# Attention scores over 64 rows: two heads in TensorE's row halves in place of stacked high and low parts

## The chip, the cores and the metric

One core of one Trainium2 chip runs the whole program. The metric is the device time of one execution in microseconds (us). The core has a matrix engine (TensorE, "PE" in the profile, with its weight loads listed apart as "PEld"), three engines for elementwise work (VectorE or DVE, ScalarE or ACT, GpSimd or POOL), and SyncE (SP), which issues most transfers. Matmuls read their operands from SBUF, which has 128 rows (partitions), and write into the banks of PSUM. In a matmul the "stationary" operand is loaded into the array first (a weight load), then the "moving" operand streams through; the contraction runs over the rows.

## The reference

The program is three transformer layers over 256 tokens of width 1024, all in float32. The change touches three groups of eight heads with 64 channels each: the sixteen heads of the neighborhood attention of the second layer (two groups), and the eight heads of the dilated attention of the third layer. Cut to what matters:

```python
# second layer: 16 heads of 64 channels
s = jnp.einsum('bqhd,bikhd->bhqik', qblk, kblk).astype(jnp.float32) * scale + bias
s = jnp.where(colmask[:, None, :], s, -jnp.inf)
p = jax.nn.softmax(s.reshape(B, H, GRID_W, kr * GRID_W), axis=-1)
...
# third layer: 8 heads of 64 channels, three causal patterns of windows
scores = jnp.einsum('bnqrhe,bnkrhe->bnrhqk', qb, kk).astype(jnp.float32) * scale
...
p = jnp.exp(scores - lse[..., None]).astype(v.dtype)
o = jnp.einsum('bnrhqk,bnkrhe->bnqrhe', p, vv)
```

With 256 tokens each head's scores are a 256 x 256 matrix, a product over 64 channels, with a bias or mask on it.

## The kernel before

**Two parts for each number.** TensorE multiplies in a rounded float32 form (F32R). To keep precision, an operand is split into a high part (rounded) and a low part (the rest): ACT writes the high part, DVE subtracts it from the source and writes the low part (`hilo`, `split`). A projection with weights then takes three matmuls: high by high, high by low, low by high.

**Tiles.** A projection (`proj_t`, `proj_sum`) leaves 256 output channels by 256 tokens as two tiles of 128 rows in `t_sum`. 128 rows are the 64 channels of two heads, a pair: head 0 in rows 0 to 63, head 1 in rows 64 to 127.

**Scores, stacked.** `q_stack` turns a pair's rows into one tile per head whose 128 rows are the 64 channels of the high part and, in the other row half, those of the low part. It takes two ACT and two DVE instructions of 64 rows for each projection. `k_stack` does the same for K, but with the high part in both halves of one tile and the low part in both halves of another; the second copies are made by four transfers that POOL issues (`nc.gpsimd.dma_start`). In `scores_stacked` a matmul of 128 rows then gives (Qhigh + Qlow) by Khigh, a second one (Qhigh + Qlow) by Klow, into the same place of PSUM. With two tiles of 128 queries a head has four matmuls. In the causal group the first query tile has only 128 keys.

**The three groups.** `heads8` runs them: c0 and c1 in `layer_odd`, d in `mixer`. It makes two projections each for K and Q, one for V, and hands `scores` to `pair_heads`, which puts three kinds of steps into a background list for each head: first (scores and softmax), second (softmax weights, transposed by TensorE), third (the product with V, for a pair). `pace` takes steps from that list while projections are written out, so that attention work stands among projection work. The product with V and all else in these groups is not changed; nor are the groups a, b and the memory heads, which use `q_stack`, `k_stack` and `scores_stacked` or `scores_full` as before.

**What sets the order.** No instruction is issued as the code is written. `Plan.record` notes each operation with its dependencies and an estimated duration from `Plan.cost`; `Plan.order` then plays the program through, and each time an engine is free it takes the ready operation with the lowest priority number. The number is the operation's place in the code plus a shift: `SHIFT = {("tensor", "mm"): 100, ("vector", "wl"): -20}` puts TensorE's projection matmuls (outputs in the PSUM tiles "mm") 100 places back. Score matmuls write to "at" tiles and get no shift. Where the two numberings meet, score and projection matmuls are taken in turn, one by one. TensorE runs its instructions in that order; `Plan.issue` emits all of them from one line, so every row of the profile bears this line (L284 before). PSUM has four "at" tiles and four "mm" tiles; a shared pool "b4" has 24 slots in SBUF, from which the Q and K tiles come too.

Of the kernel before, what the change touches and what calls it, by code (L numbers as in the profile page):

```python
# [11 lines left out]
F32R = mybir.dt.float32r  # L12
# [4 lines left out]
P = 128  # L17
S = 256
# [11 lines left out]
class Plan:  # L30
# [100 lines left out]
    def cost(self, engine, method, args, kwargs, outs, ins):  # L131

        if method == "dma_start":
            o = outs[0]
            nbytes = 4 * math.prod(o.shape)
            return (1040.0 if engine == "gpsimd" else 50.0), 950.0, nbytes
        n = math.prod(outs[0].shape[1:])
        sbuf = not any(self.mine(v) and self.tiles[v.tensor.name]["pool"].space == bass.MemoryType.PSUM for v in ins)
        col = kwargs.get("bias") is not None or isinstance(kwargs.get("scale"), bass.AP)
        accum = kwargs.get("accum_out") is not None  # L140
        if engine == "tensor":
            slow = 4.0 if args[1].dtype == F32 and method == "matmul" else 2.0 if method == "transpose" else 1.0
            if self.mine(args[2]) and args[2].tensor.name == "t_warm":
                slow = 2.0
            return max(n * slow, 256) / 2.4 + 2.4, 0.0, 0
        if engine == "scalar":
            return n / 1.2 + (93 if sbuf else 51) + 94 * col + 93 * accum, 0.0, 0
        if engine == "vector":
            if method == "tensor_reduce":
                n = math.prod(ins[0].shape[1:])  # L150
            if method in ("tensor_scalar", "tensor_copy") and sbuf:
                n /= 2
            ptr = method in ("tensor_scalar", "scalar_tensor_tensor") and isinstance(args[2], bass.AP)
            return n / 0.96 + 68 + 62 * ptr + 10 * accum, 0.0, 0
        if ALU.pow in args:
            return 300.0 + 165 * n, 0.0, 0
        if method == "memset":
            return 40.0 + n, 0.0, 0
        return 130.0 + 2.2 * n, 0.0, 0
# [148 lines left out]
class Kernel:  # L308
# [419 lines left out]
    def scores_stacked(self, q, kh, kl, spans):  # L728
# [6 lines left out]
            nc.tensor.matmul(o, q[:, t * P:(t + 1) * P], kl[:, k0:k0 + n], start=False, stop=True)  # L735
        return sc

    def scores_full(self, parts):

        sc = self.psum("at")  # L740
        for t in range(2):
            ts = slice(t * P, (t + 1) * P)
            for i, (qh, ql, kh, kl) in enumerate(parts):
                self.mm3(sc[:, t, :], qh[:, ts], ql[:, ts], kh, kl, i == 0, i == len(parts) - 1)
        return sc
# [357 lines left out]

    def heads8(self, tag, w_in, cq, ck, cv, hT, bias, out, causal=False, before=None):

        qs, ks = [], []
        for i in range(2):
            ks.append(self.k_stack(self.proj_t(w_in, ck + 256 * i, hT)))
            qs.append(self.q_stack(self.proj_t(w_in, cq + 256 * i, hT), -0.125))
        v = self.v_heads(self.proj_n(self.wide(w_in, 0, KT, cv), KT, 512, hT))  # L1110
        spans = ((0, P), (0, S)) if causal else self.FULL

        def scores(h):
            i, j = divmod(h, 4)
            return self.scores_stacked(qs[i][:, j, :], ks[i][0][:, j, :], ks[i][1][:, j, :], spans)

        if before:
            before()
        self.pair_heads(tag, 8, scores, bias, None, v, out, causal)
# [371 lines left out]
```

## Time and profile before

| | |
|---|---|
| time, median of 3 runs | 780.11 us (779.42 to 781.4) |
| the profiled execution's own time | 779.68 us |
| its span, first to last instruction | 777.9 us |
| TensorE busy | 763.1 us, 4320 matmuls recorded |
| DVE, ACT, POOL busy | 620.0, 536.8, 74.7 us |
| granted TensorE clock | 0.995 of full speed |

A group's row reads: line, engine, operation, output<-inputs by the program's names, form, count, then busy time and mean duration, then idle time before it and what ended that. In a matmul's row "128*128" are rows and columns of the stationary operand, and "128x256" is the moving one. The duration of a matmul is longer than the time for which it holds TensorE, since matmuls overlap: the pace is read from one start to the next. Timeline rows give the start, the duration of the piece, and "xN" for N alike in a row.

### The profile page before, as it was taken

What the parts mean: (1) busy time and instruction counts of PE and PEld (TensorE: products, weight loads), DVE (VectorE), ACT (ScalarE), POOL (GpSimd) and SP (SyncE); (2) the same over time, 40 slices, a digit from 0 to 9 for tenths busy, and PEclk for the clock granted to TensorE, in tenths of its full rate; (3) what the DMA queues carried; (4) which work ended last, traced back from release to release, by engine and by line L of the source; (5) the groups of instructions that cost most, each with busy time, mean ns of one, the idle gap of its engine ahead of it and who ended that gap; (6) DMA issues with size and microseconds to landing.
All of it is one profiled execution on the core that took longest, in us unless ns stands there. A gap on an engine that the chain in (4) does not pass through costs nothing.

```text
span 777.9 us, 11758 instructions
## 1 busy us (share of the span) xinstructions
PE 763.1 (98%) x4320; PEld 661.2 (85%) x4320; DVE 620.0 (80%) x1127; ACT 536.8 (69%) x1046; POOL 74.7 (10%) x105
## 2 busy tenths in 40 slices
PE   8989999999999999999999999999999999999996
PEld 7678898888888888888888898799989888888885
DVE  5999998998779889979988889976677655565554
ACT  6697987876679669757787787465556765556552
POOL 0640010000001421132011100100000000000000
PEclk9999999999999999999999999999999999999998
DMA  7796546445558855765348645356535565655631
GB/s 231 244 285 216 162 127 227 138 137 176 184 186 260 237 159 157 210 202 190 115 156 242 191 120 193 105 179 217 181 118 164 177 185 180 215 191 187 210 115 54
DMA packets 109989, 140.48 MB, mean 181 GB/s; under 512 B 3779, under 2 KB 81539, under 8 KB 109932
## 3 DMA queue, kind: packets, MB, share of 16 engines
q1 hardware_dynamic: 104460, 131.64, 52.5%
q0 software_dynamic: 5472, 8.10, 4.7%
q8 instruction: 34, 0.56, 0.3%
q14 instruction: 23, 0.19, 0.1%
HBM read 134.98 MB, written 1.06 MB: 175 GB/s over the span
## 4 chain that ended last, share of the span: by engine, by line
PE 86%; DVE 5%; issue 3%; POOL 2%; ACT 2%; DMA 1%; SPq 0%; POOLq 0%; DVEq 0%; ACTq 0%
PE t_mm L284 64%; PE t_at L284 22%; DVE t_wl L284 2%; DVE t_y L284 1%; POOL t_rrs L284 1%; POOL t_rstd L284 1%; DMA t_xT<-in_x_t_dram 1%; POOL t_ks L284 1%; ACT t_wh L284 0%; DVE t_xs L284 0%; DVE t_p L284 0%; DVE t_x L284 0%; ACT t_p L284 0%; ACT t_xg L284 0%; ACT t_mT L284 0%
## 5 line engine op out<-in xcount | busy, mean ns | idle before, releaser
L284 DVE TENSOR_TENSOR t_wl<-t_raw,t_wh 128x1024 fp32r<-128x1024 f32 (+1 forms) x237 | 288.8, 1219 | 72.6 <-ACT t_wh L284 70.9
L284 ACT ACTIVATE t_wh<-t_raw 128x1024 fp32r<-128x1024 f32 (+1 forms) x237 | 250.4, 1058 | 74.2 <-PE t_mm L284 61.3
L284 PE MATMUL t_mm<-t_mT,t_wh 128*128 128x512 f32 (+1 forms) x512 | 181.6, 394 | 0.4 <-ACT t_wh L284 0.4
L284 PE MATMUL t_mm<-t_mT,t_wl 128*128 128x256 f32 x496 | 131.9, 284 | 0.0
L284 PE MATMUL t_mm<-t_wh,t_yh 128*128 128x512 f32 x288 | 113.5, 394 | 0.0
L284 PE MATMUL t_mm<-t_wh,t_yl 128*128 128x512 f32 x288 | 112.9, 393 | 0.0
L284 PE MATMUL t_mm<-t_wl,t_yh 128*128 128x512 f32 x288 | 112.7, 391 | 0.0
L284 PEld LDWEIGHTS t_mm<-t_mT,t_wh 128*128 128x128 f32 x512 | 93.7, 188 | 14.0 <-ACT t_wh L284 0.8
L284 PEld LDWEIGHTS t_mm<-t_mT,t_wl 128*128 128x128 f32 x496 | 93.4, 189 | 6.5 <-DVE t_wl L284 0.3
L284 PE MATMUL t_at<-t_mT,t_wh 128*128 128x512 f32 (+1 forms) x256 | 85.7, 382 | 0.0
L284 ACT COPY t_sum<-t_mm 128x256 f32<-128x256 f32 x97 | 36.0, 371 | 55.6 <-PE t_mm L284 55.1
L284 PE MATMUL t_mm<-t_wh,t_gh 128*128 128x256 f32 (+2 forms) x256 | 65.9, 339 | 1.5 <-ACT t_wh L284 1.5
L284 PE MATMUL t_at<-t_mT,t_wl 128*128 128x256 f32 x240 | 63.8, 280 | 0.0
L284 PEld LDWEIGHTS t_mm<-t_wh,t_yl 128*128 128x128 f32 x288 | 54.1, 188 | 11.1
L284 PEld LDWEIGHTS t_mm<-t_wl,t_yh 128*128 128x128 f32 x288 | 54.1, 188 | 10.8
L284 PEld LDWEIGHTS t_mm<-t_wh,t_yh 128*128 128x128 f32 x288 | 54.1, 188 | 10.5 <-ACT t_yh L284 0.2
L284 PE MATMUL t_mm<-t_hT,t_wh 128*128 128x512 f32 x168 | 61.8, 400 | 1.0 <-DVE t_sum L284 1.0
L284 ACT ACTIVATE t_p<-t_p,t_st 128x256 f32<-128x256 f32 (+1 forms) x111 | 52.6, 493 | 9.6 <-DVE t_st L284 9.4
L284 POOL TENSOR_TENSOR t_rstd<-t_rstd,t_mhalf 128x2 f32<-128x2 f32 (+1 forms) x12 | 13.3, 1107 | 457.3 <-DVE t_rstd L284 457.3
L284 PEld LDWEIGHTS t_at<-t_mT,t_wh 128*128 128x128 f32 x256 | 45.8, 188 | 6.8
L284 DVE TENSOR_TENSOR t_sum<-t_mm,t_sum 128x256 f32<-128x256 f32 x97 | 40.8, 421 | 13.5 <-ACT t_sum L284 12.7
L284 PEld LDWEIGHTS t_mm<-t_wh,t_gh 128*128 128x128 f32 x256 | 45.1, 194 | 5.9 <-ACT t_wh L284 1.7
(177 smaller groups left out, 1389.1 us busy)
## 6 DMA issues: line engine op xcount, KB each, us to landing
t_raw<-in_w_in_odd_dram SPq DMA_DIRECT2D x20, 1024.0 KB, 5.2
t_raw<-in_w_up_dram SPq DMA_DIRECT2D x16, 1024.0 KB, 5.7
t_raw<-in_w_down_dram SPq DMA_DIRECT2D x16, 1024.0 KB, 5.0
t_raw<-in_w_in_dram SPq DMA_DIRECT2D x12, 1024.0 KB, 5.5
t_raw<-in_w_in_even_dram SPq DMA_DIRECT2D x10, 1024.0 KB, 5.1
t_raw<-in_w_mem_kv_dram SPq DMA_DIRECT2D x8, 1024.0 KB, 5.2
t_raw<-in_w_out_even_dram SPq DMA_DIRECT2D x6, 1024.0 KB, 5.6
t_raw<-in_w_out_odd_dram SPq DMA_DIRECT2D x6, 1024.0 KB, 5.3
```

The costliest lines, as they stand in the source:

```text
L284: f(*[self.real(v) for v in args], **{k: self.real(v) for k, v in kwargs.items()})
```

## The change

The three groups of `heads8` no longer stack. Q and K of a pair are split by `hilo` as they lie, high and low in tiles of their own, one ACT and one DVE instruction of 128 rows for each projection; Q takes two slots of the pool and K two, for all eight heads. The transfers that POOL issued for the second copies of K are gone in these groups (24 of them; the eight for a and b stay). `scores_pair` computes two heads at once: for each query tile and each of three terms (Qhigh Khigh, Qhigh Klow, Qlow Khigh) one matmul over rows 0 to 63 for the first head, and one over rows 64 to 127 for the second, alternating, each head into its own PSUM tile. The term low by low is no longer computed. A pair has twelve matmuls of 64 rows in place of eight of 128; both heads' scores are made in the step of the first head, and the second head's wait in `ready`. `Plan.cost` gets a price for such a matmul: half of the columns, at least 128.

```diff
+            if args[1].dtype == F32R and args[1].shape[0] == 64:
+                slow = 0.5
+            return max(n * slow, 128 if slow < 1 else 256) / 2.4 + 2.4, 0.0, 0
...
+    def scores_pair(self, qh, ql, kh, kl, spans):
+
+        sc = [self.psum("at") for _ in range(2)]
+        terms = ((qh, kh), (qh, kl), (ql, kh))
+        for t, (k0, n) in enumerate(spans):
+            for i, (x, y) in enumerate(terms):
+                for e in range(2):
+                    rows = slice(64 * e, 64 * e + 64)
+                    self.nc.tensor.matmul(sc[e][:, t, :n], x[rows, t * P:(t + 1) * P], y[rows, k0:k0 + n], start=i == 0,
+                                          stop=i == 2)
+        return sc
...
     def heads8(self, tag, w_in, cq, ck, cv, hT, bias, out, causal=False, before=None):
 
-        qs, ks = [], []
+        q, k = ([self.slot([P, 4, S], n) for _ in range(2)] for n in ("qs", "ks"))
         for i in range(2):
-            ks.append(self.k_stack(self.proj_t(w_in, ck + 256 * i, hT)))
-            qs.append(self.q_stack(self.proj_t(w_in, cq + 256 * i, hT), -0.125))
+            for x, c0, scale in ((k, ck, 1.0), (q, cq, -0.125)):
+                self.hilo(*(t[:, 2 * i:2 * i + 2, :] for t in x), self.proj_t(w_in, c0 + 256 * i, hT), scale)
...
+        ready = {}
+
         def scores(h):
-            i, j = divmod(h, 4)
-            return self.scores_stacked(qs[i][:, j, :], ks[i][0][:, j, :], ks[i][1][:, j, :], spans)
+            if h not in ready:
+                ready[h], ready[h + 1] = self.scores_pair(*(t[:, h // 2, :] for t in q + k), spans)
+            return ready.pop(h)
```

**Where the instructions go.** On TensorE, at the scores of the first heads of c0 (names are output<-moving,stationary; t_ks and t_qs are the K and Q tiles, t_mm a projection; the listing does not show how many rows a matmul has), before:

```order
L284 MATMUL t_at_3143<-t_ks_2837,t_qs_2937 128x256
L284 MATMUL t_at_3143<-t_ks_2848,t_qs_2937 128x256
L284 MATMUL t_at_3143<-t_ks_2837,t_qs_2937 128x256
L284 MATMUL t_at_3143<-t_ks_2848,t_qs_2937 128x256
L284 MATMUL t_mm_3150<-t_mT_2368,t_wh_3087 128x512
```

and now, in the same place:

```order
L286 MATMUL t_at_3125<-t_ks_2851,t_qs_2961 128x256
L286 MATMUL t_at_3127<-t_ks_2851,t_qs_2961 128x256
L286 MATMUL t_at_3125<-t_ks_2851,t_qs_2944 128x256
L286 MATMUL t_at_3127<-t_ks_2851,t_qs_2944 128x256
L286 MATMUL t_mm_3137<-t_mT_2368,t_wh_3071 128x512
L286 MATMUL t_at_3125<-t_ks_2862,t_qs_2944 128x256
L286 MATMUL t_mm_3137<-t_mT_2368,t_wl_3080 128x256
L286 MATMUL t_at_3127<-t_ks_2862,t_qs_2944 128x256
L286 MATMUL t_mm_3137<-t_mT_2368,t_wh_3071 128x512
```

A head's four matmuls stood together here; of the pair's twelve, eight stand together (the last four of them are shown), and the other four stand one by one between matmuls of 128 rows.

On TensorE too, later in c0, at the scores of the last pair:

```order
L286 MATMUL t_at_3447<-t_ks_2851,t_qs_2944 128x256
L286 MATMUL t_mm_3385<-t_wh_3340,t_yl_2812 128x512
L286 MATMUL t_at_3450<-t_ks_2851,t_qs_2944 128x256
L286 MATMUL t_mm_3399<-t_wh_3340,t_yh_2794 128x512
L286 MATMUL t_at_3447<-t_ks_2862,t_qs_2944 128x256
L286 MATMUL t_mm_3399<-t_wl_3358,t_yh_2794 128x512
L286 MATMUL t_at_3450<-t_ks_2862,t_qs_2944 128x256
L286 MATMUL t_mm_3399<-t_wh_3340,t_yl_2812 128x512
```

Here the two heads of a pair (tiles 3447 and 3450) take turns with the output projection of the memory heads, so the two row halves are never next to each other. Over all three groups the 144 score matmuls of 64 rows stand in 70 runs: 56 alone, and 14 runs of 2 to 12.

More of the change, by code (lines that the diff above doesn't have):

```diff
@@ L144, in cost @@
                 slow = 2.0
-            return max(n * slow, 256) / 2.4 + 2.4, 0.0, 0
+            if args[1].dtype == F32R and args[1].shape[0] == 64:
+                slow = 0.5
+            return max(n * slow, 128 if slow < 1 else 256) / 2.4 + 2.4, 0.0, 0
         if engine == "scalar":
```

## Prediction

> **What bounds the kernel now.** I read the profile's page first, then the waits of TensorE, the windows of the three stretches in which the groups of eight heads run, and last the timeline of TensorE and of its weight loads. First the page: its head, the busy time of TensorE, and the chain that ended last.
>
> ```profile
> span 777.9 us, 11758 instructions
> PE 763.1 (98%) x4320; PEld 661.2 (85%) x4320; DVE 620.0 (80%) x1127; ACT 536.8 (69%) x1046; POOL 74.7 (10%) x105
> ...
> PE 86%; DVE 5%; issue 3%; POOL 2%; ACT 2%; DMA 1%; SPq 0%; POOLq 0%; DVEq 0%; ACTq 0%
> ```
>
> TensorE (PE) is busy 98% of the span and carries 86% of the chain. A busy share says little of matmuls that are pipelined, so the waits of TensorE come next (waiter, releaser, us in total, times, longest).
>
> ```profile
> PE t_mm L284 <- ACT t_wh L284: 1.9, 2, 1.5
> PE t_mm L284 <- DVE t_wl L284: 1.6, 3, 1.0
> ...
> PE t_at L284 <- DVE t_qs L284: 0.2, 1, 0.2
> PE t_at L284 <- DVE t_y L284: 0.2, 1, 0.2
> ```
>
> The largest is 1.9 us; no row names the K tiles (t_ks) or their copies, and the Q tiles (t_qs) cost 0.2 us once. Now the windows of the stretches with the projections, scores and softmax of the groups c0, c1 and d (start:end, length, busy time of each engine).
>
> ```profile
> 222.00:290.00 68.00, 68.00 (x400) 59.68 (x399) 59.20 (x119) 52.10 (x107) 17.47 (x21) 1.00 0.72 215
> 290.00:360.00 70.00, 70.00 (x403) 60.94 (x402) 61.72 (x128) 51.15 (x104) 16.61 (x21) 1.00 0.67 194
> 408.00:478.00 70.00, 69.82 (x411) 61.05 (x412) 62.61 (x138) 55.55 (x125) 4.79 (x9) 1.00 0.63 186
> ```
>
> TensorE is busy 207.8 of these 208 us at the full clock (1.00). So what the change is worth there is what it does to TensorE's stream, and hardly anything else.
>
> **What leaves ACT, DVE and POOL.** The rows of the K and Q tiles in this part of the span (count, duration in ns min/median/max), and the rows of qm, which is split already in the form that the change adopts:
>
> ```profile
> L284 PE MATMUL t_at<-t_ks,t_qs x96: 220/281/336, 271.0 to 461.7; 128*128 128x256 f32 x80, 128*128 128x128 f32 x16
> L284 POOL DMA_DIRECT2D t_ks<-t_ks x24: 581/581/628, 242.5 to 429.7; - x24
> L284 ACT ACTIVATE t_ks<-t_sum x12: 617/628/632, 241.6 to 427.3; 64x512 fp32r<-64x512 f32 x12
> L284 DVE TENSOR_TENSOR t_ks<-t_sum,t_ks x12: 676/684/692, 242.7 to 428.6; 64x512 fp32r<-64x512 f32 x12
> ...
> L284 ACT ACTIVATE t_qs<-t_sum x12: 616/627/630, 248.7 to 434.0; 64x512 fp32r<-64x512 f32 x12
> L284 DVE SCALAR_TENSOR_TENSOR t_qs<-t_sum,t_qs x12: 684/686/690, 250.1 to 435.5; 64x512 fp32r<-64x512 f32 x12
> ...
> L284 ACT ACTIVATE t_qm<-t_sum x4: 618/625/635, 62.0 to 220.0; 128x512 fp32r<-128x512 f32 x4
> L284 DVE SCALAR_TENSOR_TENSOR t_qm<-t_sum,t_qm x4: 674/682/686, 63.0 to 220.8; 128x512 fp32r<-128x512 f32 x4
> ```
>
> Twelve projections lose half their splitting: ACT 24 x 0.63 becomes 12 x 0.63, 7.5 us less; DVE 24 x 0.685 becomes 12 x 0.68, 8.2 us less; POOL loses 24 DMA issues, 14 us. I take 0 for all three on the path, since TensorE waits 0.2 us for these tiles and there is 0.2 us of idle to win back in 208. That is also the most that this part can gain, and it cannot lose anything. Two fewer slots of the shared pool per group (four tiles for six) go the same way.
>
> **What TensorE's own stream costs.** Before, 24 heads have four score matmuls each, 96. Now twelve pairs have twelve each, 144: three terms, two query tiles, two heads. So 48 more instructions, each with its own weight load. What one costs is read from starts. The timeline of TensorE where a head's four run in a row, and where four others run one by one among projection matmuls (start, us, form):
>
> ```profile
> 271.03 0.64 PE L284 MATMUL t_at<-t_ks,t_qs 128*128 128x256 f32 x4
> 271.50 0.40 PE L284 MATMUL t_mm<-t_mT,t_wh 128*128 128x512 f32 x1
> ...
> 272.91 0.28 PE L284 MATMUL t_at<-t_ks,t_qs 128*128 128x256 f32 x1
> 273.03 0.40 PE L284 MATMUL t_mm<-t_mT,t_wh 128*128 128x512 f32 x1
> 273.27 0.28 PE L284 MATMUL t_at<-t_ks,t_qs 128*128 128x256 f32 x1
> 273.39 0.28 PE L284 MATMUL t_mm<-t_mT,t_wl 128*128 128x256 f32 x1
> ```
>
> Four start to start take 0.47 us, 0.12 each, and the lone ones too (272.91 to 273.03): today a score matmul costs the same in a row as alone. The pace of the weight loads is read where four short matmuls stand in a row early in the span (four loads and the load behind them, then TensorE's own rows; the loads are 128 columns wide, like every load of the scores):
>
> ```profile
> 21.41 0.52 PEld L284 LDWEIGHTS t_at<-t_p,t_ones 128*128 128x128 f32 x4 [0.86 <-DVE t_p L284]
> 21.85 0.19 PEld L284 LDWEIGHTS t_mm<-t_wh,t_gh 128*128 128x128 f32 x1
> ...
> 21.41 0.71 PE L284 MATMUL t_at<-t_p,t_ones 128*128 128x128 f32 x4 [0.43 <-DVE t_p L284]
> 21.88 0.47 PE L284 MATMUL t_mm<-t_wh,t_gh 128*128 128x512 f32 x1
> 22.19 0.39 PE L284 MATMUL t_mm<-t_wl,t_gh 128*128 128x512 f32 x1
> ```
>
> Four loads take 0.44 us, so one per 0.11 us is the load path's pace. It is the floor for a matmul that brings a load of its own, whatever its stream takes; the 16 narrow causal ones (128 columns) also stand at about 0.11. Before: 80 x 0.12 + 16 x 0.11 = 11.3 us. After, at the load pace: 144 x 0.11 = 15.8 us, **+4.5 us**. Bounds: 0.12 each would be +6.0; if the two row halves load and stream at once, a pair costs one place, 0.055 each, 7.9 us, a gain of 3.4. Nothing in this trace shows two halves at work at once, while loads of 128 columns one behind the other are in every window, so I take 0.11.
>
> The second cost is the change of the array's shape, from 128 rows to 64 and back. One place of this trace has a matmul of another shape, the small one of the window bias (33 rows, 8 columns, recorded as two passes). Its group, an ACT instruction that the reading needs, and the timeline of the loads and of TensorE around it:
>
> ```profile
> L284 PE MATMUL t_at<-t_tanh,t_rb 33*8 33x512 f32 x2 | 1.0, 586 | 0.7 <-POOL t_sink L284 0.7
> ...
> 19.41 1.06 ACT L284 ACTIVATE t_wh<-t_raw 128x1024 fp32r<-128x1024 f32 x1 [0.24 <-DMA t_raw<-in_w_in_even_dram]
> ...
> 26.23 0.12 PEld L284 LDWEIGHTS t_at<-t_tanh,t_rb 33*8 33x8 f32 x2 [1.08 <-POOL t_sink L284]
> ...
> 26.26 1.01 PE L284 MATMUL t_at<-t_tanh,t_rb 33*8 33x512 f32 x2 [0.69 <-POOL t_sink L284]
> 27.20 0.50 PE L284 MATMUL t_mm<-t_wh,t_gh 128*128 128x512 f32 x1
> 27.54 0.40 PE L284 MATMUL t_mm<-t_wl,t_gh 128*128 128x512 f32 x1
> ...
> 27.20 0.19 PEld L284 LDWEIGHTS t_mm<-t_wh,t_gh 128*128 128x128 f32 x1 [0.86 <-ACT t_hT L284]
> ```
>
> The pair of passes lasts 1.01 us and one of them 0.59, so they start 0.42 apart and stream until 26.26 + 2 x 0.42 = 27.10. The next load starts at 27.20, 0.1 us behind the end of the stream; at 21.85 above, between matmuls of one shape, it began 0.27 us before the recorded end of the row of four (21.41 + 0.71). And the matmul behind it holds TensorE for 0.34 us (27.20 to 27.54) where one of 512 columns takes 0.24 (273.03 to 273.27), so 0.1 of load lies open. One change of shape: 0.1 + 0.1 = 0.20 us. The profile names ACT as the releaser of that load, but the tile t_wh that this matmul reads was written by the ACT instruction at 19.41, so I read the 0.86 us as the wait for the passes to leave the array.
>
> How many such changes there are follows from the order. Of the 144 instructions 56 stand alone between matmuls of 128 rows, as the second excerpt on the change shows, and 88 stand in 14 rows of 2 to 12. That makes 70 runs, 140 changes. The way in is not shown by any row: the load at 26.23 waited for POOL. From 0 to the price of the way out, I take the latter, since the array holds matmuls of the other shape in both directions: 140 x 0.20 = **+28.0 us**. Upper bound for a change: the whole tail of a matmul (0.28 recorded less 0.12 of pace) and a whole recorded load of 0.19, 0.35 us, +49. Lower: 0.
>
> The Trainium skill says, in "TensorEngine Tiling (Array Packing)", Key Properties, that changing the tiling mode, and not only the tile, drains TensorE. It gives no price; by it the way in costs as well, and the sum is the one that I take. The one change of shape in this trace agrees (0.1 us behind the end of the stream).
>
> The sum against the profiled execution of 779.68 us: +4.5 + 28.0 = +32.5, 812.2; the median of the runs is 780.11, 0.43 above it, so **812.6 us**.
>
> **Rivals.** (1) The change of shape costs half: only one direction empties the array, or the open load is all. 4.5 + 140 x 0.10 = +18.5, 798.6 us. For it: the way in is unseen. Against it: the order puts as many ways in as out.
>
> (2) It costs nothing and the loads still go one by one: +4.5, 785 us. For it: the row at 26.26 differs also in its 8 columns and its float32 type, so its emptying may belong to the columns. Against it: the row of four ahead of 21.85 is float32 too (both operands are float32 in the code) and shows none.
>
> (3) It costs nothing and the halves run side by side inside the 14 rows: 42 pairs and 4 left over at 0.11 and 56 lone ones at 0.12, 11.8 us for 11.3: 780.5 us, no change. The 56 lone ones have no partner to run beside.
>
> (4) The other side: half the rows make load and stream half as long for every one of the 144, lone ones too, and the change of shape is free: 144 x 0.06 = 8.6 us for 11.3, -2.7, 777.4 us. This is what the planner's new cost for such matmuls says. It decides only if a change of shape costs less than 2.7 / 140 = 0.02 us, a tenth of what the trace shows once. The Trainium skill speaks for (3) and (4) where it says, in "TensorE: Matmul & The Clock Gate", The mechanism, that loads overlap running matmuls when the row groups differ; no run here shows it so far.
>
> **How the numbers follow.** The forecast has 0.58 (0.05 of that above 820 us, toward the upper price), (1) 0.15, (2) 0.10, (3) 0.08, (4) 0.09. The range 781 to 820 leaves out (4), half of (3) and that upper end. A measurement of this kernel tells about 0.3%, 2.3 us, from no change: the forecast, (1) and (2) are slower, 0.83; (3) the same, 0.08; (4) faster, 0.09.
>
> **What would show it.** Right: lone score matmuls of 64 rows take 0.4 to 0.5 us from the matmul before to the one after, instead of 0.12; the loads around them start only behind the end of the stream; rows of eight or twelve step at about 0.11 us; the three stretches grow by some 10 us each and the rest of the span stays. The load groups of t_at<-t_ks,t_qs count 144, ACT and DVE are 7 to 8 us lighter, and TensorE's waits name no new tile. Wrong: lone ones at 0.12 us with loads ahead of them (rivals 2 to 4), starts of two halves a few ns apart (3), or a new wait of TensorE for score banks (t_at), since a pair now takes two of four at once, which would add to any of these.

## The result and the profile after

The changed kernel takes 813.48 us (median of 4 runs, 812.86 to 814.21); before it was 779.76 us beside it. The ratio is 1.0428, with a 95% interval of 1.0411 to 1.0445: 34 us slower. The profile's page of the changed kernel, its head, the busy times and the granted clock in 40 slices:

```profile
span 812.1 us, 11774 instructions
...
PE 796.9 (98%) x4368; PEld 670.9 (83%) x4368; DVE 618.5 (76%) x1117; ACT 528.6 (65%) x1032; POOL 58.8 (7%) x81
...
PEclk9999999999999999999999789999999999999998
```

TensorE is "busy" for 34 us more with only 48 more matmuls, 0.7 us for each. DVE, ACT and POOL are lighter (618.5 for 620.0, 528.6 for 536.8, 58.8 for 74.7). New are the 7 and the 8 in the row of the clock, some 450 to 475 us into the span.

The score matmuls and their loads in the three groups, in the view by tile (durations min/median/max):

```profile
L286 PEld LDWEIGHTS t_at<-t_ks,t_qs x144: 182/183/285, 271.7 to 493.3; 64*128 64x128 f32 x144
L286 PE MATMUL t_at<-t_ks,t_qs x144: 268/331/579, 271.7 to 493.3; 64*128 64x256 f32 x120, 64*128 64x128 f32 x24
```

They are the 144 that were forecast, now of 64 rows ("64*128"). Where lone ones stand between projection matmuls, TensorE's timeline in c0 reads (start, duration, form):

```profile
273.12 0.38 PE L286 MATMUL t_mm<-t_mT,t_wl 128*128 128x256 f32 x1
273.43 0.38 PE L286 MATMUL t_at<-t_ks,t_qs 64*128 64x256 f32 x1
273.74 0.50 PE L286 MATMUL t_mm<-t_mT,t_wh 128*128 128x512 f32 x1
274.17 0.38 PE L286 MATMUL t_at<-t_ks,t_qs 64*128 64x256 f32 x1
274.48 0.38 PE L286 MATMUL t_mm<-t_mT,t_wl 128*128 128x256 f32 x1
```

and the loads of weights in the same place:

```profile
273.43 0.18 PEld L286 LDWEIGHTS t_at<-t_ks,t_qs 64*128 64x128 f32 x1
273.74 0.19 PEld L286 LDWEIGHTS t_mm<-t_mT,t_wh 128*128 128x128 f32 x1
274.17 0.18 PEld L286 LDWEIGHTS t_at<-t_ks,t_qs 64*128 64x128 f32 x1 [0.25 <-issue]
274.48 0.19 PEld L286 LDWEIGHTS t_mm<-t_mT,t_wl 128*128 128x128 f32 x1
```

Every step that took 0.12 us before takes 0.31 (273.12 to 273.43, 273.43 to 273.74), and that of 512 columns 0.43 (273.74 to 274.17) where it took 0.24. Each load starts in the same hundredth of a microsecond as its own matmul, so nothing was loaded ahead. Against 0.12 that is 0.19 for each change of the array's shape, on the way in as on the way out. As an estimate, a step of 0.31 is a load of 0.11 (the pace of the loads before), a stream of 0.11 and 0.09 that is left for emptying; no row shows load and emptying apart.

Where eight stand in a row, the same timeline shows something else:

```profile
271.39 0.39 PE L286 MATMUL t_mm<-t_wh,t_mT 128*128 128x512 f32 x1
271.71 0.74 PE L286 MATMUL t_at<-t_ks,t_qs 64*128 64x256 f32 x8
272.38 0.50 PE L286 MATMUL t_mm<-t_mT,t_wh 128*128 128x512 f32 x1
```

Eight take 0.67 us, with the load and the emptying in it; at 0.11 each they alone would take 0.88. The two row halves do run side by side.

### The profile page after: what moved, and what is told of

It is laid out like the page before. It is cut to its first block, busy times and chain, and to the rows that moved or that the text cites. A ratio compares the mean times of both kernels' runs of the same rounds, so it can differ in the third digit from the quotient of the medians.

```text
span 812.1 us, 11774 instructions
## 1 busy us (share of the span) xinstructions
PE 796.9 (98%) x4368; PEld 670.9 (83%) x4368; DVE 618.5 (76%) x1117; ACT 528.6 (65%) x1032; POOL 58.8 (7%) x81
## 4 chain that ended last, share of the span: by engine, by line
PE 89%; DVE 4%; issue 3%; POOL 2%; DMA 1%; ACT 1%; SPq 0%; POOLq 0%; ACTq 0%; DVEq 0%
PE t_mm L286 66%; PE t_at L286 23%; DMA t_raw<-in_w_in_even_dram 1%; DVE t_wl L286 1%; DVE t_y L286 1%; POOL t_rrs L286 1%; POOL t_ks L286 1%; POOL t_rstd L286 0%; DVE t_p L286 0%; DVE t_mT L286 0%; DVE t_sum L286 0%; ACT t_wh L286 0%; DVE t_tanh L286 0%; SPq L286 0%; DVE t_yl L286 0%
## 5 line engine op out<-in xcount | busy, mean ns | idle before, releaser
L286 PE MATMUL t_mm<-t_mT,t_wh 128*128 128x512 f32 (+1 forms) x512 | 184.5, 400 | 0.0
L286 PE MATMUL t_mm<-t_mT,t_wl 128*128 128x256 f32 x496 | 134.2, 288 | 0.1
L286 ACT ACTIVATE t_p<-t_p,t_st 128x256 f32<-128x256 f32 x112 | 52.9, 492 | 17.1 <-DVE t_st L286 16.6
L286 PEld LDWEIGHTS t_at<-t_mT,t_wl 128*128 128x128 f32 x240 | 45.3, 189 | 3.2
```

Source lines behind the costliest of these rows:

```text
L286: f(*[self.real(v) for v in args], **{k: self.real(v) for k, v in kwargs.items()})
```

## The experiments

All times are medians, beside runs of the kernel before on the same chip (779.10 us; for the last experiment 779.69).

**Which part is the change of shape.** The first keeps the 144 matmuls and gives them a priority that lets them follow one another.

```diff
     def scores_pair(self, qh, ql, kh, kl, spans):
         sc = [self.psum("at") for _ in range(2)]
+        self.nc.bias = -400
...
+        self.nc.bias = 0
         return sc
```

> The same 144 score matmuls of 64 rows, but with a priority that lets a pair's or a head's matmuls follow one another: 23 runs between matmuls of 128 rows in place of 70, so 46 changes of the array's shape in place of 140. Theory (each change of shape empties the array and opens a load, 0.195 us): 144 x 0.11 + 46 x 0.195 - 11.3 = +13.5 us, about 793 us. Rival A (the 64-row matmuls themselves are slow, whatever their neighbours): unchanged, about 813 us. Rival B (two halves side by side pay once they stand together): a pair would cost 0.11 us, 72 x 0.11 + 9.0 - 11.3 = +5.6, about 785 us.

Measured: 790.18 us, ratio 1.0146 (1.0121 to 1.017), +11.1 us. Two thirds of the loss are gone with two thirds of the changes of shape, which rules out rival A. Part of that is a lowered clock in group d, which comes up below and which this run doesn't have. The theory gave 2.4 us too much: in its trace 28 of the 144 matmuls start within 0.01 us of the one before, so they run side by side, and the theory counted none of them. In c0 and c1 most heads still follow one after the other here instead of in turn (one score bank comes free before the other), so this run doesn't tell rival B apart.

The second leaves the order alone and takes away the shape.

```diff
-            if args[1].dtype == F32R and args[1].shape[0] == 64:
+            if self.short:
...
-                    rows = slice(64 * e, 64 * e + 64)
-                    self.nc.tensor.matmul(sc[e][:, t, :n], x[rows, t * P:(t + 1) * P], y[rows, k0:k0 + n], start=i == 0,
+                    self.nc.short = True
+                    self.nc.tensor.matmul(sc[e][:, t, :n], x[:, t * P:(t + 1) * P], y[:, k0:k0 + n], start=i == 0,
                                           stop=i == 2)
+                    self.nc.short = False
```

> The changed kernel with the same order on every engine, but each of the 144 score matmuls reads all 128 rows of the pair's tiles. The two heads of a pair are thereby not kept apart: both get the sum of the two heads' scores. Theory: no change of shape is left, 120 x 0.12 + 24 x 0.11 - 11.3 = +5.7 us, about 785.5 us, full clock. Rival A (the order or the number of matmuls makes the loss): about 813 us. Rival C (part of the loss is a new wait for score banks or for ACT and DVE): above 787 us.

Measured: 784.55 us, ratio 1.0071 (1.0048 to 1.0094), +5.45 us. The order is the changed kernel's, the number of matmuls too, and 29 of the 34 us are gone, the lowered clock among them. What is left is about what the theory gave for 48 more matmuls, 5.7. So the loss comes from the 64 rows among 128, and not from the planner's order, from banks or from other engines: rivals A and C fall.

**What the lighter engines are worth.** The cheap split alone, with the old number of matmuls:

```diff
-            if h not in ready:
-                ready[h], ready[h + 1] = self.scores_pair(*(t[:, h // 2, :] for t in q + k), spans)
-            return ready.pop(h)
+            return self.scores_stacked(q[0][:, h // 2, :], k[0][:, h // 2, :], k[1][:, h // 2, :], spans)
```

> Only the cheap split is kept: ACT and DVE instructions of 128 rows, no transfers for second copies of K, and the scores with as many matmuls of 128 rows as before (two per head and query tile, on the pair's tiles as they lie). The heads of a pair are not kept apart and the term of the low part of Q is left out. Theory: what ACT, DVE and POOL save is covered by TensorE, so within 0.3% of the time before, 779 to 781 us. Rival: it is worth up to 2.5 us, 777.5 us.

Measured: 778.48 us, ratio 0.9991 (0.9981 to 1.0002). In the profiles ACT is 7.3 us lighter than before, DVE 4.8 and POOL 14.4, with 24 transfers fewer, and that gives at most 0.2%: they were covered.

**The groups apart, and the clock.** Group d stacked as before, with c0 and c1 changed, and the reverse. The first of the two edits (the other calls `heads8_stacked` for c0 and c1, and `heads8` for d):

```diff
+    def heads8_stacked(self, tag, w_in, cq, ck, cv, hT, bias, out, causal=False, before=None):
+        ...
-        self.heads8("d", w_in, 0, 512, 1024, hT, lambda h: b, lambda f, o: finish("attn", f, o), True)
+        self.heads8_stacked("d", w_in, 0, 512, 1024, hT, lambda h: b, lambda f, o: finish("attn", f, o), True)
```

> Group d stacked as before, c0 and c1 as in the change: 96 matmuls of 64 rows in 45 runs, 90 changes of shape. Theory: 96 x 0.11 + 16 x 0.12 + 16 x 0.11 - 11.3 + 90 x 0.195 = +20.5 us, about 800.5 us, and if the half clock seen in group d comes from the gaps of its own runs it is gone. Rival A, by number of matmuls alone: two thirds of the loss, 802 us. Rival D (the loss is mainly the half clock of group d): about 790 us.

> Only group d as in the change; c0 and c1 stacked as before. 48 matmuls of 64 rows, most of them alone, some 24 runs between matmuls of 128 rows. Theory (changes of shape alone): about 50 x 0.195 + 0.5 = +10, 789.5 us. With the half clock that the changed kernel's profile shows in this group (17 us, worth about 5 us): about 795 us, and the clock row below full in the same place. If the losses of the groups add up, this run and e3_d_stacked together lose as much as the whole change, 34 us.

Measured: 796.86 us with d stacked (ratio 1.0232, 1.0203 to 1.0262, +17.8), and 797.31 us with d alone changed (1.0221, 1.0194 to 1.0248, +18.2). Together 36.0 us, for 34 of the whole change. Neither run met its theory: the first lies 3.6 us below it, since 29 of the 96 matmuls run side by side with the one before and the theory counted none (with them it is +17.8), and rivals A (802) and D (790) miss as well; the second lies 2.3 above its 795. But d has 48 of the 144 matmuls and 25 of the 70 runs, and it costs half. The clock in 40 slices, of the first kernel (d stacked):

```profile
PEclk9999999999999999999999999999999999999998
```

and of the second (d alone changed):

```profile
PEclk9999999999999999999999799999999999999999
```

In these runs the lowered clock comes with d changed. In the changed kernel the windows of that place read (start:end, length, busy of TensorE, loads, DVE, ACT, POOL, then the clock, the DMA share and GB/s):

```profile
443.00:449.00 6.00, 6.00 (x28) 3.92 (x26) 2.68 (x4) 2.80 (x4) 0.00 (x0) 1.00 0.61 196
449.00:456.00 7.00, 7.00 (x19) 5.13 (x20) 3.48 (x13) 2.28 (x6) 0.00 (x0) 0.51 0.11 37
456.00:463.00 7.00, 7.00 (x25) 3.95 (x23) 3.67 (x6) 2.59 (x7) 0.00 (x0) 0.98 0.47 150
463.00:473.00 10.00, 10.00 (x22) 6.50 (x22) 3.65 (x15) 2.92 (x9) 0.00 (x0) 0.50 0.09 18
```

For 17 us TensorE got half its clock. 41 matmuls started there; at the pace of 443 to 449 (28 in 6 us) they would take 8.8 us, at that of 456 to 463 (25 in 7 us) 11.5, so the half clock cost 5.5 to 8 us. Set step by step against the same steps at full clock it is 7.7, again an estimate. The run of d alone gives the same from the other side: 18.2 measured, 50 x 0.195 + 0.5 = 10.2 for the changes of shape, 8 left. Its trace has 13.7 us of half clock in d, and 3.4 us more some 29 us into the span, long before any of these matmuls.

**The planner's new price**, taken back alone:

```diff
-            if args[1].dtype == F32R and args[1].shape[0] == 64:
-                slow = 0.5
-            return max(n * slow, 128 if slow < 1 else 256) / 2.4 + 2.4, 0.0, 0
+            return max(n * slow, 256) / 2.4 + 2.4, 0.0, 0
```

> The change without the planner's new price for matmuls of 64 rows. The score matmuls stand in 70 runs again, 58 of them single matmuls. Theory (the runs decide): as the changed kernel, 813 us within 3. Rival P (the price, by making the planner believe in short scores, spoils the order): below 805 us.

Measured: 814.80 us, ratio 1.0449 (1.0422 to 1.0476). Same number of runs, same loss: the price isn't the cause. The trace of this run has the half clock not in d alone: it stands at 0.50 from 307.0 to 310.4 us too, in c0, right behind a stretch in which lone score matmuls and projection matmuls take turns.

**What side by side is worth.** Here, besides the priority of the first run, a pair's first matmul also waits for the second bank, so that all twelve alternate. A "place" is what one matmul takes of TensorE in a row of its like, 0.117 us.

```diff
+        self.nc.bias = -400
...
                     self.nc.tensor.matmul(sc[e][:, t, :n], x[rows, t * P:(t + 1) * P], y[rows, k0:k0 + n], start=i == 0,
                                           stop=i == 2)
+                    if t == i == e == 0:
+                        self.nc.ops[-1]["uses"].add(sc[1].tensor.name)
+        self.nc.bias = 0
```

> As e1_together, but the first matmul of a pair also waits for the second head's score bank, so that a pair's twelve matmuls stand together and always alternate between the row halves: 14 runs, 28 changes of shape, 72 adjacent pairs. Theory, new form (each change of shape costs 0.195 us, and two neighbours in different row halves cost one place of 0.117 us, as the steps of 0.003 and 0.117 us in e1_together and in the changed kernel suggest): 72 x 0.117 + 28 x 0.195 - 11.3 = +2.6 us, 0.6 less for what ACT, DVE and POOL save: about 781 us. Rival L, as in the prediction (the loads allow one matmul per 0.11 us, side by side or not): 144 x 0.11 + 28 x 0.195 - 11.3 = +10, 789 us. Rival W (a pair that waits for two banks holds up TensorE): above 784 us with waits named t_at.

And its twin, the same edit with both heads in the same half (the second head then gets the first one's scores):

```diff
-                    rows = slice(64 * e, 64 * e + 64)
+                    rows = slice(0, 64)
```

> The order of e8_pairs on every engine, but both heads of a pair read rows 0 to 63, so no two neighbours are in different row halves (the second head of each pair gets the first head's scores). Theory, new form: 144 x 0.117 + 28 x 0.195 - 11.3 = +11, about 789.5 us, 8.4 us above e8_pairs. Rival L: as e8_pairs, within 1 us.

Measured: 782.06 us alternating (ratio 1.0032, 1.002 to 1.0043, +3.0) and 790.33 us in one half (1.013, 1.0106 to 1.0153, +11.2). The difference is 8.3 us, where 72 places of 0.117 us are 8.4 (in the trace 67 of the 72 neighbours start side by side, 7.8). The first is 1 us above its theory: TensorE waits 1.2 us once for a Q tile there. Rival W would have been above 784. TensorE's timeline at the first eight of a pair, alternating:

```profile
253.43 0.40 PE L286 MATMUL t_mm<-t_mT,t_wh 128*128 128x512 f32 x1
253.76 0.74 PE L286 MATMUL t_at<-t_ks,t_qs 64*128 64x256 f32 x8
254.43 0.39 PE L286 MATMUL t_mm<-t_mT,t_wl 128*128 128x256 f32 x1
```

and in one half:

```profile
253.26 0.40 PE L286 MATMUL t_mm<-t_mT,t_wh 128*128 128x512 f32 x1
253.59 1.21 PE L286 MATMUL t_at<-t_ks,t_qs 64*128 64x256 f32 x8
254.73 0.38 PE L286 MATMUL t_mm<-t_mT,t_wl 128*128 128x256 f32 x1
```

0.67 us for eight against 1.14: four places less, at 0.117 each. Two neighbours in different halves cost one place, weight loads included, and rival L falls.

**With as few changes of shape as the banks allow.** Two pairs at a time, 24 matmuls together, again with the priority of the first run:

```diff
+        sc = [self.psum("at") for _ in range(4)]
+        self.nc.bias = -400
...
+                        if first is None:
+                            op["uses"].update(s.tensor.name for s in sc)
+                            first = op["i"]
+                        else:
+                            op["deps"].setdefault(first, 0.0)
```

> As e8_pairs, but two pairs at a time: their 24 matmuls stand together and wait for all four score banks. 7 runs, 14 changes of shape, 72 adjacent pairs of row halves. Theory: 72 x 0.117 + 14 x 0.195 - 11.3 = -0.2 us, 0.6 less for what ACT, DVE and POOL save: 778.3 us, at the edge of what can be told from the kernel before. Rival W (waiting for all four banks holds back transposes and the products with V, which need banks too, and leaves TensorE idle): above 782 us, with more waits of TensorE than 7.6 us.

Measured: 779.11 us beside 779.69, ratio 0.9994 (0.9983 to 1.0005), -0.6 us: close to the theory's -0.8, no difference that can be told, and no sign of rival W (above 782). The busy time of the 120 wide score matmuls, in the groups by form, of the changed kernel:

```profile
L286 PE MATMUL t_at<-t_ks,t_qs 64*128 64x256 f32 x120 | 27.9, 350 | 0.0
```

of the pairs that alternate:

```profile
L286 PE MATMUL t_at<-t_ks,t_qs 64*128 64x256 f32 x120 | 10.5, 297 | 1.2 <-ACT t_qs L286 1.2
```

and of two pairs at a time:

```profile
L286 PE MATMUL t_at<-t_ks,t_qs 64*128 64x256 f32 x120 | 8.9, 288 | 0.0
```

The same 120 matmuls stand for 27.9, 10.5 or 8.9 us of TensorE, by their neighbours alone, but for the part that the half clock has in the first. No version beat the kernel before by more than a measurement tells.

## Why the prediction was right, and where it was not

The forecast was 812.6 us, and 813.48 was measured. Its main step holds; two smaller ones were wrong by about the same amount in opposite directions, so the closeness of the total is partly luck.

- **The bound.** TensorE's stream was the right place to look: with the 128 rows back and all else kept, 29 of 34 us are gone.
- **ACT, DVE and POOL at nothing.** Right: 0.6 us, within the interval of none.
- **140 changes of shape at 0.20 us, +28.0.** Right. The timeline shows 0.19 on both sides of a lone matmul, the count of 70 runs came from the order, and 140 x 0.195 = 27.3. That the way in costs as much as the way out, for which the prediction had no row, is now seen; the rule of the Trainium skill that was weighed there, in "TensorEngine Tiling (Array Packing)", Key Properties, agrees with the estimate of 0.09 us of emptying at each change. The runs follow the count: 46 changes +11.1 us, 28 changes +3.0, 14 changes -0.6, where the first has few alternating neighbours and the others alternate nearly throughout. Counted in the traces, these three runs have 116, 77 and 72 places, the twin in one half 144; places x 0.117 + changes x 0.195, less the 11.3 of before and 0.6, give +10.6, +2.6, -0.7 and +10.4, where +11.1, +3.0, -0.6 and +11.2 were measured.
- **144 matmuls at the load path's 0.11, +4.5.** Wrong in size. Loads for the two halves don't queue behind each other: the 70 runs take 102 places (42 neighbours share one), 102 x 0.117 = 11.9 for 11.3 us before, +0.6. The row that I leaned on shows loads of 128 rows only. The mechanism of rival (3) was real, as the Trainium skill has it in "TensorE: Matmul & The Clock Gate", The mechanism; the eight in 0.67 us agree. It was just far too small against the changes of shape.
- **The half clock was not foreseen.** 5.5 to 8 us in group d, for which no term stood in the sum. So +0.6 + 27.3 + 5.5 to 8 = 33.4 to 35.9, less 0.6 for the lighter engines; 33.7 measured by the medians.
- **Rivals.** (1) and (2) fall with the price on both sides; (3) had the row halves right and the change of shape wrong; (4) falls with the lone matmuls' 0.31 us. The condition of (4), a change of shape below 0.02 us, is missed by a factor of ten.
- **What would show it.** The loads behind the stream and the lone steps came as written, and c0 and c1 grew by 17.8 us together, some 20 by the forecast. The rows of eight did not step at 0.11, and d grew by 16.6 (813.48 less 796.86), not by 10. ACT is 8.2 us lighter as written, but DVE only 1.5: its rows for K and Q are 8.3 lighter, while other rows took longer (t_gh 9.6 us for 7.1). TensorE's waits show nothing new for the scores.

## What to carry to other kernels

Matmuls of 64 rows in alternating row halves do share a place, but a change between 64 and 128 rows costs almost two such places, so the gain depends on how many stand together: count the runs in the final order, not the matmuls. Here 24 at a time broke even, 12 lost 0.3%, and runs that are mostly single matmuls lost 4%. A planner that prices such matmuls by the instruction can't see this, since the cost lies between neighbours.

## What was not expected of the hardware

TensorE's clock fell to half in group d, at 449.0 and 462.7 us, although the profile shows it busy without a gap ahead of that (6.00 of 6.00 and 7.00 of 7.00 us, 28 and 25 matmuls started). The Trainium skill, in "TensorE: Matmul & The Clock Gate", Part 1, ties the half clock to at least one idle window of about 3.4 us; no such idle time shows here. With the same matmuls of d standing together the clock stayed full (mean 0.996 for the pairs, 0.995 before, 0.984 for the change).

It isn't a matter of d alone, since the run with the old price shows it once in c0; in the changed kernel the same kind of alternation in c0 kept the full clock. An estimate from starts and column counts (0.117 us for 256 columns, matmuls side by side counted once): between 20 and 760 us the clock drops eight times in three of the eleven traces, and in the 3.4 us ahead of each drop the streams fill only 0.43 to 0.49 of the time. Of over two thousand other such stretches at full clock six are as poor. So little streaming goes with the drop, in c0 and d without any wait of TensorE in the profile; that it is the cause, and where the limit lies, is not shown.
